# A one-core encoder block: three of five token tiles get their expert gates by one-hots instead of two, and four other rules of the order change

## The chip, the cores and the metric

The kernel runs on one core of one Trainium2 chip. The metric is the device time of one execution in microseconds, from the runs of the program on the chip; the profile is one more such execution, recorded by the hardware profiler. TensorE is PE here, VectorE DVE, ScalarE ACT, GpSimd POOL and SyncE SP, as the profile calls them.

## The reference, cut to what matters

One layer over 1,024 tokens of width 1,024. First a token-mixing sub-layer, then a layer of single-neuron experts, then a norm.

```python
n = modulate(rms_norm(h, g_norm1), shift1, scale1)
a_val, a_gate, u, v, gate_a, gate_b = split(n @ w_in)
z = conv_causal_31(a_val * sigmoid(a_gate)) + dw_b        # per channel
y_a = silu(layer_norm(z)) @ w_conv_out
mixed = einsum("gij,bnjgc->bnigc", w_masked, layer_norm(v)) + b_s
y_b = (u * mixed) @ w_sgu_out
h = h + gate1 * ((sigmoid(gate_a) * y_a + sigmoid(gate_b) * y_b) @ w_out)

n2 = modulate(rms_norm(h, g_norm2), shift2, scale2)
# 8 heads, 2 x 128 keys: top 16 of each half, top 16 of their sums
gate = softmax(s); e_idx = i1 * 128 + i2                  # 128 experts a token
a = einsum("td,tkd->tk", n2, expert_u[e_idx])
y = einsum("tk,tkd->td", gelu(a) * gate, expert_v[e_idx])
out = rms_norm(h + gate2 * y, g_final)
```

The shifts, scales and gates (`shift1` ... `gate2`) come from a small product of a conditioning row with `w_ada`, in twelve chunks of 512 columns.

## The kernel before, in words

**Tokens.** There are eight tiles of 128 tokens. The front half of the program runs over them in three blocks, of 3, 2 and 3 tiles (0 to 2, 3 and 4, 5 to 7). A block goes through a fixed list of weight products on PE, each of 24 matmuls of 128 x 128 weights with 384 or 256 token columns: for the first block `w_v`, then eight times `w_av`, `w_ag`, `w_u`; eight times `w_gb`, `w_sgu`; eight `w_ga`; eight `w_conv`; eight `w_out`. Then come the next block's `w_v`, and eight times the next block's `w_av`, `w_ag` and two of this block's 16 query products `w_q`, each followed by small score products. Weights are split into a high and a low part so that a float32 product takes three fast matmuls; the low part is made once, stored, and loaded again for the later blocks.

**The convolution** of a block is a generator (`conv`, held by `Conv`, line 961) that runs beside the products: 31 taps a channel tile on DVE (line 174), a mean over the channels by eight matmuls with `onesd`, a subtraction, squares, eight more such matmuls, a root, and then the swish and the split into high and low parts, which `w_conv` needs. In the last two blocks the last `NPT` = 4 taps of a channel tile are matmuls on PE with diagonal matrices `dg` that ACT makes.

**Experts.** Tiles 0 to 4 (`NDT` = 5) are dense: for each of 128 rows of 128 experts PE multiplies all 640 tokens by all experts' `expert_u`, DVE multiplies by a gate that is zero where the expert was not chosen, and PE multiplies by `expert_v`. Tiles 5 to 7 gather: for each token's 128 experts POOL gathers the rows of `expert_u` and then of `expert_v`, 384 + 384 gathers of 512 KB, and DVE makes 384 dot products and 384 scaled sums. The gathers run beside the dense part.

**Gates.** The dense tiles need their gates as a table, expert by token, in memory. `route` (line 341) finds a tile's 128 experts a token on DVE. For the first `NDD` = 3 tiles the table `g_a` is filled with zeros by SP, and `scatter` (line 554) lets POOL add the gates one column of 128 tokens at a time: 128 indirect transfers a tile, in 8 heads of 16, where a head waits for the landing of the tile's head before. The tiles' heads take turns. For the other `NOH` = 2 tiles the table is made by one-hots (class `Scatter`): 32 groups a tile, each of two comparisons and one product on DVE, twelve matmuls of 128 x 128 on PE (`pg`) and four copies on ACT, stored to `g_b`.

**What sets the order.** Nothing is scheduled by the chip or by a compiler: the program is written by a planner (`Plan`, line 60) that keeps a clock for each engine and records instructions as it goes. Work in the front line is recorded in program order. Tasks have a due time. Background generators (`pl.add`) are stepped in between the matmuls, the one with the lowest number first (`g[3]`: -1 free, 0 urgent, 1 the rest), as long as DVE's planned clock is not too far ahead. Each engine then takes its instructions strictly in the order they were recorded and waits on semaphores. SP takes nearly all loads and stores; in the last block's score products the last two stores go through POOL (`pl.late`).

**Other names.** `split_w` (line 669) casts a weight tile and calls for the next loads (`fetch_w`, `fetch_lo`). `mix_tables` loads the 128 x 128 mixing matrix `ws` and its bias row `tg` for one channel group. `ada` (line 741) makes one of the chunks of the conditioning product, in eight steps on DVE with four loads `aw`; chunks 6 to 9 must be done before the second norm's transposes. `routes` (line 1237) routes the tiles one after the other. `fence` waits for all scatters before the tables are read.

Of the kernel before, what the change touches and what calls it, by code (L numbers as in the profile page):

```python
# [9 lines left out]
BF16 = mybir.dt.bfloat16  # L10
I32 = mybir.dt.int32
# [19 lines left out]
BLOCKS = [(0,3),(3,2),(5,3)]  # L31
NDD = 3
TC = 32
# [13 lines left out]
NZ = 4  # L47
NPT = 4
LEAD = 1.0
# [252 lines left out]
def build(ctx, tc, I, O):  # L302
# [146 lines left out]
    class Scatter:  # L449
# [32 lines left out]
        def onehots(self, n):  # L482
# [3 lines left out]
            o1 = self.sb.tile([P, P, NTK], BF16, name="o1", tag="o1", bufs=2)  # L486
            o2 = self.sb.tile([P, P, NTK], BF16, name="o2", tag="o2", bufs=2)
            yield max([pl.ready(x, None, True) for x in (o1, o2)] + [pl.ready(iB), pl.ready(gB)])
# [75 lines left out]
    def scatter(gate, at):  # L564
# [6 lines left out]
        for h in range(H):  # L571
            now = []
            for k in range(h * K, (h + 1) * K):
# [7 lines left out]
                tc.add_to_no_dep_group("sc", i)  # L581
                pl.op("pool", 1.9, [], [gate, at])
                now.append(i)
# [85 lines left out]
    def split_w():  # L669
        if raws:  # L670
# [5 lines left out]
            def work():  # L676
                if old:
                    yield pl.ready(raw)
                    f = pl.acopy(hi, raw)
                    fetch_w()  # L680
                    fetch_lo()
                    yield max(f, pl.ready(lo))
                    return
# [280 lines left out]
    class Conv:  # L964


        def __init__(self, b, nn):
            self.N, self.nn = BLOCKS[b][1] * P, nn
            self.zs, self.done, self.free, self.out = {}, [], [], []
            self.zc = big("zc")  # L970
            self.gen = pl.add(conv(self.zc, self.zs, self.done, self.N, self.free, self.out, b + 1), True)

        def glu(self, j):
# [18 lines left out]
    def front(b, nn, v, cv):  # L992
# [26 lines left out]
        if b == 0:  # L1019
            cv = Conv(b, nn)  # L1020
        for j in range(J):
            if b == 0:
                cv.glu(j)
            tabs = mix_tables(j)
            pu = product(nh, nl, N)
            pend.append((j, pu) + tabs)
            if len(pend) > 1:
                pl.flush(1)
                mix(*pend.pop(0))
        pl.flush(1)  # L1030
        mix(*pend.pop(0))
# [210 lines left out]
    def routes():  # L1242
        for t in range(T // P):
            while t >= NDD and len(sct.routed) > 1 or len(heads) < min(t, NDD) - 3:
                yield pl.now + 1.0
            while t >= NDT and sct.made < NOH * sct.NQ:
                yield max(pl.now, pl.t["dve"]) + 1.0
            gate, i1f, i2f = r = [rp.tile([P, P], F32, name=n, tag=n, bufs=4 if n == "gate" else 2)
                                  for n in ("gate", "i1f", "i2f")]
            yield from route(rp, t, r)  # L1250
            if t < NDD:
                at = gsb.tile([P, P], I32, name="at", tag="at", bufs=4)
                pl.stt(i1f, i2f, float(P), i1f, OP.mult, OP.add)
# [461 lines left out]
```

## Time and profile before

| | |
|---|---|
| median of three runs | 3425.19 us (3420.99 to 3430.82) |
| the profiled execution's own time | 3423.22 us |
| its span from the first to the last instruction | 3421.1 us |
| PE busy | 3086.7 us, 90% |
| DVE busy | 2804.2 us, 82% |
| ACT busy | 1148.2 us, 34% |
| POOL busy | 1674.1 us, 49% |
| moved by DMA | 995.88 MB, 291 GB/s on average |

The front half ends and the dense half begins near 1,510 us. A busy time is a sum over the whole span; what a stage is worth is read from that stage. The busy time of PE is partly modelled, since its matmuls overlap. In a row of the profile `out<-in` names tiles, and in brackets stands how long the engine was idle ahead of it and what ended that.

### The profile page before, as it was taken

To read this page: it belongs to the slowest core of one execution; us is meant where nothing else is said; L and a number is where in the kernel's file an instruction comes from. 1 tells how busy PE (TensorE), PEld (TensorE's weight loads), DVE (VectorE), ACT (ScalarE), POOL (GpSimd) and SP (SyncE) were. 2 spreads that over 40 slices of the span, in tenths; PEclk is the share of its full clock that TensorE was granted. 3 is DMA by queue.
4 is the path that set the end of the run, shared out by engine and by line. 5 is a ranking of instruction groups with operands and counts; after the bars stand their busy time and mean duration, and the time that the engine had idled before them with its cause. 6 is when DMAs were issued, how large, how long until landed. Compare 5 with 4: busy or idle time off the path is not lost.

```text
span 3421.1 us, 49027 instructions
## 1 busy us (share of the span) xinstructions
PE 3086.7 (90%) x17598; PEld 2810.1 (82%) x17598; DVE 2804.2 (82%) x5741; ACT 1148.2 (34%) x1978; POOL 1674.1 (49%) x1549
## 2 busy tenths in 40 slices
PE   7969859888999969878999999999999999999991
PEld 4969749887798858777999999888889999999891
DVE  3799648777888847427999999899999998999998
ACT  4223444446543345533222222222222223222221
POOL 0000000027899999981232556566665554565663
PEclk9989989999999979989999999999999999999996
DMA  6969977879997758875676999999999998999997
GB/s 245 313 226 351 324 263 278 296 261 341 268 276 214 212 115 242 222 222 156 223 251 206 346 326 358 331 350 355 346 338 351 345 352 302 356 349 360 339 350 286
DMA packets 474036, 995.88 MB, mean 291 GB/s; under 512 B 87640, under 2 KB 247256, under 8 KB 473792
## 3 DMA queue, kind: packets, MB, share of 16 engines
q1 hardware_dynamic: 307776, 589.43, 49.7%
q0 software_dynamic: 166016, 403.32, 36.0%
q8 instruction: 138, 2.26, 0.3%
q14 instruction: 106, 0.87, 0.1%
HBM read 881.89 MB, written 110.71 MB: 290 GB/s over the span
## 4 chain that ended last, share of the span: by engine, by line
PE 36%; DVE 19%; DMA 18%; POOL 14%; issue 9%; ACT 3%; SPq 1%; DVEq 0%; ACTq 0%; POOLq 0%
PE ps L144 12%; POOL g_a L575 12%; PE pa L144 12%; PE pk L144 7%; DVE ya L174 6%; DMA raw<-in_v 5%; PE pr L144 5%; DMA w<-in_v,e 3%; DVE scr L174 2%; DVE yb L161 1%; DVE zc L174 1%; DVE vl L161 1%; DVE wlo L161 1%; DVE odd L174 1%; POOL w L1416 1%
## 5 line engine op out<-in xcount | busy, mean ns | idle before, releaser
L575 POOL DMA_INDIRECT g_a<-gate,at x384 | 654.9, 1705 | 842.3 <-DVE at L168 747.2
L1416 POOL DMA_INDIRECT w<-in_u,e x384 | 483.7, 1260 | 542.4 <-DVE scr L174 368.5
L144 PE MATMUL pa<-n2h,uh 128*128 128x320 f32 x2016 | 626.2, 311 | 39.6 <-ACT ge L195 37.3
L1416 POOL DMA_INDIRECT w<-in_v,e x384 | 485.5, 1264 | 343.1 <-DVE ya L174 243.4
L144 PE MATMUL pa<-n2l,uh 128*128 128x320 f32 x2016 | 625.9, 310 | 0.7 <-DVE n2l L161 0.7
L144 PE MATMUL pa<-n2h,ul 128*128 128x320 f32 x2016 | 625.9, 310 | 0.0
L174 DVE SCALAR_TENSOR_TENSOR ya<-w,aa,ya 128x1024 f32<-128x1024 f32 x381 | 489.1, 1284 | 23.7 <-DMA w<-in_v,e 18.3
L174 DVE SCALAR_TENSOR_TENSOR scr<-w,n 128x1024 bf16<-128x1024 f32 x384 | 469.3, 1222 | 12.1 <-DMA w<-in_u,e 4.6
L144 PEld LDWEIGHTS pa<-n2h,uh 128*128 128x128 f32 x2016 | 381.4, 189 | 52.5 <-ACT ge L195 40.8
L203 ACT CAST whi<-raw 128x1024 fp32r<-128x1024 f32 x264 | 276.7, 1049 | 387.4 <-PE ps L144 87.1
L144 PEld LDWEIGHTS pa<-n2l,uh 128*128 128x128 f32 x2016 | 381.2, 189 | 10.4 <-DVE n2l L161 1.1
L144 PEld LDWEIGHTS pa<-n2h,ul 128*128 128x128 f32 x2016 | 381.2, 189 | 0.0
L144 PE MATMUL ps<-nh,whi 128*128 128x384 f32 (+1 forms) x1024 | 352.1, 344 | 24.2 <-DVE z L161 10.7
L144 PE MATMUL ps<-nh,wlo 128*128 128x384 f32 (+1 forms) x1024 | 343.1, 335 | 7.8 <-DVE wlo L161 6.1
L144 PE MATMUL ps<-nl,whi 128*128 128x384 f32 (+1 forms) x1024 | 341.8, 334 | 1.6 <-DVE nl L161 1.6
L195 ACT ACTIVATE ge<-pa 128x320 f32<-128x320 f32 x249 | 108.6, 436 | 662.5 <-PE pa L144 662.5
L203 ACT CAST hh<-ge 128x320 fp32r<-128x320 f32 x250 | 115.0, 460 | 549.3 <-DVE ge L161 549.3
L144 PE MATMUL pk<-vh,hh 128*128 128x512 f32 x768 | 298.8, 389 | 0.0
L144 PE MATMUL pk<-vl,hh 128*128 128x512 f32 x768 | 298.8, 389 | 0.0
L144 PE MATMUL pk<-vh,hl 128*128 128x512 f32 x768 | 298.8, 389 | 0.0
L574 POOL MEMSET pad<- 128x1 f32 x384 | 274.3, 714 | 0.0
L144 PE MATMUL ps<-gh,whi 128*128 128x256 f32 (+1 forms) x704 | 223.8, 318 | 13.3 <-ACT gh L203 9.2
(252 smaller groups left out, 6663.1 us busy)
## 6 DMA issues: line engine op xcount, KB each, us to landing
raw<-in_uT SPq DMA_DIRECT2D x128, 512.0 KB
raw<-in_v SPq DMA_DIRECT2D x128, 512.0 KB
g_a<-zt SPq DMA_DIRECT2D x24, 1024.0 KB
raw<-in_w_q SPq DMA_DIRECT2D x48, 512.0 KB
gt<-g_a SPq DMA_DIRECT2D x32, 640.0 KB
aw<-in_w_ada SPq DMA_DIRECT2D x32, 512.0 KB
wlo<-lo_d_w_q SPq DMA_DIRECT2D x32, 512.0 KB
g_b<-st SPq DMA_DIRECT2D x32, 512.0 KB
```

Of the source, the lines that this page charges most:

```text
L144: self.nc.tensor.matmul(ps, w, x, start=start, stop=stop)
L161: self.nc.vector.tensor_tensor(out=out, in0=a, in1=b, op=op)
L174: self.nc.vector.scalar_tensor_tensor(out, a, s, b, op0=op0, op1=op1, **kw)
L195: self.nc.scalar.activation(out, a, func, **kw)
L203: self.nc.scalar.copy(out, a)
L574: nc.gpsimd.memset(pad, 0.0)
L575: i = nc.gpsimd.indirect_dma_start(out=g_1, out_offset=bass.IndirectOffsetOnAxis(ap=at[:, k:k + 1], axis=0), in_=gate[:, k:k + 1], in_offs ...
L1416: nc.gpsimd.indirect_dma_start(out=w, out_offset=None, in_=I["v" if ph else "u"], in_offset=bass.IndirectOffsetOnAxis(ap=ra[a][0][:, k:k + ...
```

## The change

Seven edits, in one diff:

- the gates of tiles 0 and 1 come by additions, those of tiles 2, 3 and 4 by one-hots (`NDD` 2, so `NOH` 3); the planner's price of one addition goes from 1.9 to 2.1, and `at` has two buffers instead of four;
- all 31 taps run on DVE in every block (`NPT` 0);
- one of the one-hot tiles, `o2`, has three buffers instead of two;
- where a weight's low part is loaded rather than made, the next loads are recorded when the planned cast has ended, and no longer with the cast;
- the background generators of the convolution, and of the routing from the second tile on, get the number 0.5 instead of 0;
- the mixing tables of group j + 1 are asked for after product j and before the next group's products.

```diff
-NDD = 3
+NDD = 2
...
-NPT = 4
+NPT = 0
...
-            o2 = self.sb.tile([P, P, NTK], BF16, name="o2", tag="o2", bufs=2)
+            o2 = self.sb.tile([P, P, NTK], BF16, name="o2", tag="o2", bufs=3)
...
-                pl.op("pool", 1.9, [], [gate, at])
+                pl.op("pool", 2.1, [], [gate, at])
...
                 if old:
                     yield pl.ready(raw)
-                    f = pl.acopy(hi, raw)
+                    yield pl.acopy(hi, raw)
                     fetch_w()
                     fetch_lo()
-                    yield max(f, pl.ready(lo))
+                    yield pl.ready(lo)
                     return
...
             self.gen = pl.add(conv(self.zc, self.zs, self.done, self.N, self.free, self.out, b + 1), True)
+            self.gen[3] = 0.5
...
+        tabs = mix_tables(0)
         for j in range(J):
             if b == 0:
                 cv.glu(j)
-            tabs = mix_tables(j)
             pu = product(nh, nl, N)
             pend.append((j, pu) + tabs)
             if len(pend) > 1:
                 pl.flush(1)
                 mix(*pend.pop(0))
+            if j + 1 < J:
+                tabs = mix_tables(j + 1)
...
+            rg[3] = 0.5 if t else 0
             yield from route(rp, t, r)
             if t < NDD:
-                at = gsb.tile([P, P], I32, name="at", tag="at", bufs=4)
+                at = gsb.tile([P, P], I32, name="at", tag="at", bufs=2)
```

The order that comes out differs in many places. Three of them follow.

PE, second block, where the first eight `onesd` matmuls of its convolution stand (`zc,onesd`). In this block `gh` and `gl` are the normed input's two parts. Before, they stand inside the product `w_gb4`:

```order
L144 MATMUL ps<-gh,whi 128x256
L144 MATMUL ps<-gl,whi 128x256
L144 MATMUL ps<-gh,wlo 128x256
L144 MATMUL ps<-zc,onesd 128x256 x8
L144 MATMUL ps<-gh,whi 128x256
```

Now they stand behind the last `w_ga` product, directly followed by the eight for the squares (`ts,onesd`), and the rows after those are `w_conv0`:

```order
L144 MATMUL ps<-gh,whi 128x256
L144 MATMUL ps<-gl,whi 128x256
L144 MATMUL ps<-gh,wlo 128x256
L144 MATMUL ps<-zc,onesd 128x256 x8
L144 MATMUL ps<-ts,onesd 128x256 x8
L144 MATMUL ps<-nh,whi 128x256
L144 MATMUL ps<-nl,whi 128x256
```

The tail of the convolution moved by 15 products, to the place where its result is wanted next. In the third block the matmuls for the squares moved in the same way, from `w_ga2` and `w_ga3` to the end of `w_ga7`.

PE, third block, in the query products, at the scores (`sk,qT`) between two of them. Before:

```order
L144 MATMUL ps_14724<-nl_14046,whi_14638 128x384
L144 MATMUL ps_14724<-nh_14045,wlo_14552 128x384
L144 MATMUL ps_14756<-sk_14502,qT_14719 128x128 x3
L144 MATMUL ps_14764<-nh_14045,whi_14681 128x384
L144 MATMUL ps_14764<-nl_14046,whi_14681 128x384
```

Now a group of twelve one-hot matmuls begins after the first matmuls of the product (its first two stand here):

```order
L144 MATMUL ps_15004<-sk_14593,qT_14865 128x128 x3
L144 MATMUL ps_15011<-nh_13575,whi_14733 128x384
L144 MATMUL ps_15011<-nl_13576,whi_14733 128x384
L144 MATMUL ps_15011<-nh_13575,wlo_14615 128x384
L144 LDWEIGHTS o2_14970
L144 MATMUL pg_15016<-so_15002,o2_14970 128x128
```

37 of the 96 groups now stand among the query products `w_q0` to `w_q11`, where none stood; 50 stand among `w_conv` and `w_out` (53 before), 5 among the second block's query products (none before), and 4 from `w_sgu4` to `w_ga7` (10, from `w_ga3` on, before; one more stood in the first `w_conv` and is counted in the 53).

DVE, third block, the write of tile 4's gates (`gate<-s,z`), with the semaphores it waits for; `DMASW` are those of POOL's transfers. Before, in product `w_ga3`, with one-hots of tile 3 ahead of it and behind it:

```order
L161 TENSOR_TENSOR o_11640<-iorep,iB 128x512
L161 TENSOR_TENSOR o_11641<-iorep,iB 128x512
L187 TENSOR_REDUCE z<-s 128x8 [waits Activation_49]
L183 RECIPROCAL z<-z 128x8 [waits DVE_49]
L161 TENSOR_TENSOR gate<-s,z 128x128 [waits DMASW4_49,DMASW3_49,DMASW5_49,DMASW2_49,DMASW6_49,DMASW1_49,DMASW7_49,DMASW0_49,DVE_49]
L161 TENSOR_TENSOR so<-o_11640,gB 128x1536
```

Now, in product `w_ga7`:

```order
L161 TENSOR_TENSOR s<-s,m 128x128 [waits DVE_49]
L187 TENSOR_REDUCE z<-s 128x8 [waits Activation_49]
L183 RECIPROCAL z<-z 128x8 [waits DVE_49]
L161 TENSOR_TENSOR gate<-s,z 128x128 [waits DMASW4_49,DMASW3_49,DMASW5_49,DMASW2_49,DMASW6_49,DMASW1_49,DMASW7_49,DMASW0_49,DVE_49]
L161 TENSOR_TENSOR so<-o_10872,gB 128x1536
```

The wait is still there: the four gate buffers go round, and tile 4 takes the one that tile 0's scatters read. It moved back by four products. In POOL's queue tile 0's last head is number 14 of 24 heads before (224 transfers with all before it) and number 12 of 16 now (192 transfers).

## Rows read from the trace of the kernel before

**Rows 1.** The chain of waits, first the stretch from 1100 to 1260 us, then from 1260 to 1560 us: its shares by line.

```profile
by line: POOL g_a L575 85.7%; issue 9.7%; POOL pad L574 6.2%
...
by line: POOL g_a L575 78.0%; issue 9.6%; POOL pad L574 5.6%; DMA g_a<-gate,at 2.4%; PE pa L144 1.8%; DMA sc_d<-so 1.1%; PE pr L144 0.7%; ACT L195 0.4%; ACT vh L203 0.3%; ACT ge L195 0.1%; ACTq L203 0.0%; POOLq L575 0.0%; POOLq L229 0.0%
```

**Rows 2.** Busy time by stretch: from and to, length, then busy us (and instructions) of PE, PE's weight loads, DVE, ACT and POOL, the granted clock of PE, the share of the DMA engines, GB/s.

```profile
857.00:1037.00 180.00, 172.14 (x1039) 157.79 (x1037) 150.60 (x446) 91.39 (x158) 162.16 (x156) 0.98 0.92 273
1037.00:1182.00 145.00, 137.78 (x761) 131.51 (x760) 129.34 (x522) 46.32 (x71) 131.03 (x150) 0.98 0.80 219
1182.00:1261.00 79.00, 40.35 (x256) 36.64 (x255) 26.91 (x55) 32.70 (x69) 71.36 (x84) 0.76 0.43 78
1261.00:1407.00 146.00, 144.84 (x987) 128.18 (x985) 106.14 (x199) 83.01 (x256) 132.41 (x148) 1.00 0.82 233
1425.00:1508.00 83.00, 79.57 (x468) 78.89 (x468) 18.04 (x71) 27.25 (x45) 74.80 (x88) 0.95 0.96 274
1508.00:1552.00 44.00, 12.03 (x62) 11.14 (x60) 11.82 (x27) 11.23 (x15) 30.97 (x36) 0.62 0.45 102
1552.00:1850.00 298.00, 295.20 (x1653) 269.20 (x1654) 278.75 (x892) 87.67 (x141) 61.87 (x53) 0.99 0.67 215
...
2050.00:2550.00 500.00, 489.09 (x2713) 442.64 (x2712) 459.32 (x634) 126.53 (x208) 309.14 (x238) 0.99 0.96 349
2550.00:3348.00 798.00, 794.33 (x4441) 721.84 (x4440) 749.01 (x968) 211.31 (x345) 464.69 (x369) 1.00 0.96 344
3348.00:3421.00 73.00, 2.06 (x9) 1.33 (x8) 59.99 (x59) 10.83 (x22) 27.82 (x23) 0.55 0.72 265
```

**Rows 3.** Who waited for whom between 1150 and 1260 us: engine, tile and line, what it waited for, us in total, times, the longest.

```profile
DVE gate L161 <- DMA g_a<-gate,at: 41.1, 1, 41.1
...
PE pg L144 <- DVE so L161: 38.6, 1, 38.6
```

**Rows 4.** The same between 1495 and 1600 us.

```profile
ACT vh L203 <- DMA sc_d<-so: 30.5, 1, 30.5
...
PE pa L144 <- ACT ge L195: 29.7, 1, 29.7
```

**Rows 5.** POOL in order of time, at its last scatter: start, length, engine, line, operation.

```profile
1544.58 1.56 POOL L575 DMA_INDIRECT g_a<-gate,at  x1 [0.19 <-issue]
1545.55 2.25 POOL L229 DMA_DIRECT2D sc_d<-so  x2
```

**Rows 6.** The instructions on the table `g_a`: shortest, median and longest in ns, first and last start.

```profile
L575 POOL DMA_INDIRECT g_a<-gate,at x384: 1556/1563/9224, 750.3 to 1544.6; - x192
```

**Rows 7.** POOL's instructions on `g_a` alone, by stretch: length, busy us (and how many), granted clock of PE, DMA share, GB/s.

```profile
750.00:850.00 100.00, 73.95 (x46) 0.97 1.01 331
850.00:950.00 100.00, 80.54 (x44) 0.97 0.92 275
950.00:1050.00 100.00, 86.78 (x44) 1.00 0.92 270
1050.00:1150.00 100.00, 84.45 (x52) 0.97 0.80 221
```

**Rows 8.** Groups of instructions between 1261 and 1407 us, in which 53 groups of one-hots ran: how many, busy us, mean ns of one, idle time ahead of them and what ended it.

```profile
L144 PE MATMUL pg<-so,o 128*128 128x128 bf16 x648 | 84.7, 297 | 0.8 <-DVE so L161 0.5 <-ACT st L203 0.3
...
L203 ACT COPY st<-pg 128x128 f32<-128x128 f32 x224 | 62.9, 441 | 48.2 <-PE pg L144 25.4 <-DMA g_b<-st 22.0 <-ACT st L203 0.3
...
L161 DVE TENSOR_TENSOR so<-o,gB 128x1536 bf16<-128x1536 bf16 x53 | 50.5, 954 | 0.0
L161 DVE TENSOR_TENSOR o<-iorep,iB 128x512 bf16<-128x512 bf16 x105 | 42.9, 423 | 30.1 <-PE pg L144 30.1
```

**Rows 9.** The instructions on `dg` alone, by stretch: length, busy us (and how many) of PE, PE's weight loads and ACT, then clock, DMA share and GB/s.

```profile
500.00:700.00 200.00, 13.22 (x56) 10.31 (x56) 10.21 (x32) 0.96 0.83 290
700.00:900.00 200.00, 1.89 (x8) 1.44 (x8) 0.00 (x0) 0.95 0.91 295
900.00:1160.00 260.00, 21.95 (x64) 11.82 (x64) 11.22 (x32) 0.99 0.87 250
```

**Rows 10.** Groups on DVE between 504 and 1160 us: half of the taps of a channel tile, with 384 and with 256 columns.

```profile
L174 DVE SCALAR_TENSOR_TENSOR zc<-z,cw,zc 128x384 f32<-128x384 f32 x104 | 63.8, 614 | 10.0 <-ACT zc L195 10.0
...
L174 DVE SCALAR_TENSOR_TENSOR zc<-z,cw,zc 128x256 f32<-128x256 f32 x104 | 49.9, 480 | 16.3 <-ACT zc L195 16.3
```

**Rows 11.** All engines in order of time at the end of the first block's convolution, behind its `w_ga7`; the last row is the first matmul of `w_conv0`.

```profile
338.80 5.32 PE L144 MATMUL ps<-zc,onesd 128*128 128x384 f32 x16
...
345.32 5.43 PE L144 MATMUL ps<-ts,onesd 128*128 128x384 f32 x16 [1.20 <-ACT ts L195]
...
351.40 2.55 DVE L183 RECIPROCAL ts<-ts 128x384 f32<-128x384 f32 x1 [3.43 <-ACT ts L195]
...
354.58 4.89 ACT L195 ACTIVATE zc<-zc,cols 128x384 f32<-128x384 f32 x8 [1.91 <-DVE zc L161]
...
359.93 0.69 PE L144 MATMUL ps<-gh,whi 128*128 128x384 f32 x1 [9.18 <-ACT gh L203]
```

**Rows 12.** DVE in order of time at the end of the first block: the end of chunk 8 of the conditioning product, the first and the last step of chunk 9.

```profile
443.88 0.16 DVE L174 SCALAR_TENSOR_TENSOR mcol<-ps,cols 128x4 f32<-128x4 f32 x1 [1.85 <-PE ps L154]
...
464.17 0.49 DVE L166 TENSOR_SCALAR acc<-aw,cT 128x512 f32<-128x512 f32 x1 [10.57 <-DMA aw<-in_w_ada]
...
474.23 0.16 DVE L174 SCALAR_TENSOR_TENSOR mcol<-ps,cols 128x4 f32<-128x4 f32 x1 [1.21 <-PE ps L154]
```

## The prediction, made before the changed kernel ran

> **What bounds the kernel now.** I read the chain of waits first, because it names the work that ends last. From 1100 us to 1551 us it runs almost wholly through POOL's scatters into `g_a` [rows 1]. Then I cut the span into stages [rows 2]. From 1261 us on, PE is busy 99% of most stretches, so a PE instruction added there costs its whole time. Two stretches stand out: 1182 to 1261 us, with PE busy 40.35 of 79 us, and 1508 to 1552 us, with 12.03 of 44 us. The waits tell why. In the first, DVE's gate of tile 4 waits 41.1 us for tile 0's scatters, which read the buffer it wants, and PE waits 38.6 us for the one-hot product queued behind it on DVE [rows 3]. In the second, ACT's `vh` waits 30.5 us for a store of scores, and PE 29.7 us for ACT [rows 4]; POOL issues that store only behind its last scatter, at 1545.55 us [rows 5]. Between 857 and 1182 us PE, weight loads, DVE and the DMA engines are all nearly full [rows 2]: 15 of 325 us is all PE has idle there. In the last 73 us PE is done; DVE works 60.0 us of them.
>
> So the kernel is bound by PE, with two holes of 68 us together that the additions make. The change takes a third of the additions away and gives PE matmuls for them.
>
> **The change part by part.** The sum goes by the profiled execution's 3423.2 us; the median of the runs is 2.0 us above it.
>
> *The wait for tile 4's gate.* The 384 transfers begin at 750.3 us [rows 6]; 186 are issued by 1150 us, then 0.52 a us [rows 7]. Tile 0's last is number 224: 38 more take 73 us, to 1223 us, and with a landing of 7.2 us (2.4% of the 300 us of chain, [rows 1]) 1230 us. The wait of 41.1 us before that began near 1189 us. Now the last is number 192: 6 more take 12 us, so it lands near 1169 us. DVE reaches the gate four products later; one product is 24 matmuls of three parts, 72 at 0.170 us (79.57 us by 468, [rows 2]), so 12 us, and even if only 16 us of work lies between, it is there near 1205 us. That leaves 36 us of margin: −38.6 us. Bounds: −44 (the slower clock, 0.76 mean in that stretch, comes back too) to −30 (a weight load or the norm is late next).
>
> *The store on POOL.* 256 transfers end 70 after number 186, that is 135 us after 1150, near 1285 us. Nothing stands ahead of the store when the scores are done: −29.7 us. Next late is the start of the dense loads, so −10 is the other bound; below −30 nothing can go.
>
> *One-hots for tile 2.* 32 groups more, each 12 matmuls. The 648 matmuls of such groups took 84.7 us beside other products, 0.131 us each [rows 8], where the count of loaded weights equals that of matmuls. So 32 × 12 × 0.131 = +50.2 us of PE. Is any of it hidden? 37 groups stand in the query products, where PE is busy 79.57 of 83 us [rows 2], so almost none. A group also takes 2 × 0.423 + 0.954 = 1.8 us of DVE and four copies of 0.28 us (62.9 us by 224) of ACT [rows 8]; for 37 groups 67 us of DVE and 41 us of ACT, in a stage where DVE had 18.0 and ACT 27.3 of 83 us [rows 2]. They fit beside PE, given that the stage grows by 58 us. Bounds: +25 if half goes into gaps of PE that the loads make (PE sits idle for 3 us of 83 while the DMA share is 0.96), +67 if the matmuls cost a third more among products whose weights also change each time. I take the row.
>
> *No taps on PE.* `dg` matmuls took 13.2, 1.9 and 22.0 us of PE [rows 9], 37 us. The 22.0 fall into the part from 900 us where PE paces: they go whole. Of the other 15.1 I count 3, because there PE waits for weights: −25 us. Bounds −37 to −10. On DVE, 32 taps more at 256 columns and 32 at 384 cost 32 × 0.480 + 32 × 0.614 = 35 us [rows 10]; DVE is busy 280 of the 325 us from 857 to 1182 us [rows 2], and loses ten groups' 18 us from that part, so they fit, if tightly.
>
> *The convolutions' tails.* In the second and third block the `onesd` matmuls now stand where the first block's stand: behind the last `w_ga`, with nothing recorded between them and `w_conv`. There PE was idle 1.20 us before the squares and 9.18 us before the first product [rows 11]. For 384 columns I take the 10, for 256 columns 8: +18 us. Bounds 0 (the rest of DVE's work happens to be done) to +28 (DVE is behind with the taps, and PE waits for the last of them).
>
> *Chunk 8 of the conditioning product.* Its loads stand later (from `w_out3` to `w_out7`), and its rest and chunk 9 are drained together before the second norm. The end of chunk 8 to the end of chunk 9 took 30 us, with 10.57 us of it for one load [rows 12]. Part of that lay there before; I take +8. Bounds 0 to +25.
>
> *The rest* I put at 0: eight zero fills fewer, the weight loads queued at the cast's end, the tables of one group ahead, the third `o2`, two `at`, the two generators' number, and the order of the gathers. The loads are off PE's chain where PE is 99% busy, and the stretch from 857 us can give back its 15 us at the most [rows 2]. Bounds: −25 (that, and 10 us of the first block) to +15 (the first weights arrive later behind what is queued ahead).
>
> Sum: −38.6 − 29.7 + 50.2 − 25 + 18 + 8 = −17.1, so 3406.1 us profiled and 3408 us as a median. Half the widths between the bounds (7, 10, 21, 14, 14, 12, 20) put together as independent errors, by the root of their squares, give 39 us if every one is at its bound; about half of that is my guess for most cases, so the forecast's own range is 3388 to 3428 us.
>
> **Rivals.**
>
> *1. The query products run at the one-hots' chain.* A group is a chain: comparisons and a product on DVE (1.8 us), matmuls, copies on ACT, and only three `o2`. PE takes the next group's matmuls in its order and stops if DVE has not finished. If PE waits the whole of DVE's 1.8 us in each of the 37 groups, 67 us come on top, 3475 us; with half, 3441 us. It decides from 0.46 us a group, which makes up the 17 us. Against it: with 53 groups in 146 us PE lost only 0.5 us to `so` and 0.3 us to `st` [rows 8]. For it: in that stretch the groups had products of 384 columns between them as here, but no score products with their copies on ACT. Chance 0.14.
>
> *2. The additions stay slow for longer, and the gate's wait survives.* They ran at 44 to 46 in 100 us up to 1050 us and at 52 after that [rows 7], and taps run on DVE while they are slow; with all taps on DVE that time lengthens. At 44 in 100 throughout, number 192 is issued at 750 + 436 = 1186 us and lands near 1194 us: still 11 us before DVE comes. Only at 41 in 100 (two tiles' heads in turn, not three, each waiting for its own tile's landing) is it 1218 us, landing near 1225 us, a wait of 20 us, 3428 us; in between, 3408 to 3428 us. Against it: 52 in 100 ran from 1050 us while DVE was 129 of 145 us busy [rows 2]. Chance 0.10. The Trainium skill, in "SBUF — State Buffer", section "Who interferes with whom", says that a DVE instruction with both inputs in SBUF contends with a GpSimd instruction that reads SBUF, and that the one behind stands still for the whole instruction of the other. The taps have two such inputs. By that rule all of the stretch with taps would go at the slow pace, which is the 44 in 100 above, so the rule alone leaves the forecast where it is; the trace's two paces agree with it but do not show that it is the cause.
>
> *3. The tail shrinks and the loads flow.* In the first 298 us of the dense half POOL issued only 53 instructions and the DMA share was 0.67; later it is 0.96 [rows 2]. The routing of tiles 6 and 7 moved far behind, so gathers can start at once. If those of the end have then landed before they are wanted, the tail falls from 73 us to DVE's 60.0 us in it, −13, and with the loads' 15 us of the stretch from 857 us it is 3380 us; with the tail alone 3395 us. Against it: 30 of 384 sums still stand behind the last dense piece, 31 before. Chance 0.13.
>
> **How the numbers follow.** Forecast 0.63, rivals 0.14, 0.10 and 0.13. A change of under 0.3%, 10.3 us, cannot be told from none, so faster is below 3414.9 us and slower above 3435.5 us. Of the forecast's 0.63 I put 0.41 below, 0.18 within and 0.04 above. Rival 1 gives 0.01 within and 0.13 above; rival 2 gives 0.03, 0.06 and 0.01; rival 3 gives 0.13 below. Together 0.57 faster, 0.25 same, 0.18 slower. The range for 8 times in 10 takes in rival 3's 3380 us and rival 1's half case: 3374 to 3442 us.
>
> **What would show it.** Right: no wait of `gate` on `g_a` above 5 us; no wait of `vh` on `sc_d`; the last scatter before 1300 us; the front half's end some 15 us earlier, the dense part and the tail unchanged; PE's `pg` matmuls some 50 us longer in sum; near 10 us of idle PE before each `w_conv0`. Rival 1 shows as PE waiting for `so` or `st` in the query products; rival 2 as the wait of `gate` left over; rival 3 as a tail under 65 us. The forecast fails above all if DVE, with 35 us more taps, falls behind from 857 to 1182 us: then PE waits for the convolution's tail far longer than 10 us and the gain is gone.

## The result, and the profile after

The changed kernel takes 3407.49 us (median of 8 runs, 3396.44 to 3418.14), the kernel before in the same set 3424.66 us (8 runs). The ratio is 0.9949, with a 95% interval of 0.9931 to 0.9967. The profiled execution's span is 3405.0 us, 16.1 us less than the 3421.1 us of before. The prediction was 3408 us and "faster".

A sum can be right with wrong terms, so the first question is where in the program the 16.1 us came up. The two traces have the same list of weight products, and the start of each product's first matmul can be laid side by side. The table is worked out from the PE rows of both traces. The last column says what lies in the step and, in brackets, what the prediction had put there. Its terms are PE's time from the start of a matmul to the start of the next one, with idle time counted by itself; the `onesd` matmuls in it are those of the convolutions' tails, which stand in a later step than before.

| start of | before, us | after, us | after − before | step, and the prediction's term |
|---|---|---|---|---|
| 5th `w_v` of the second block | 482.2 | 501.2 | +18.9 | chunk 8 drained: +19, of it idle +13 (+8) |
| first `w_ga`, second block | 768.9 | 767.3 | −1.6 | −20: `dg` gone −12, `onesd` moved on −6, other −2 (0) |
| first `w_conv`, second block | 795.2 | 807.4 | +12.2 | +14: `onesd` moved here +7, PE idle behind the tail +7 (+8) |
| first `w_u`, third block | 1036.9 | 1047.7 | +10.8 | −1: 5 groups added +7, `dg` gone −11, slower matmuls behind the tail +4 |
| first `w_ga`, third block | 1168.6 | 1165.4 | −3.2 | −14: `dg` gone −7, `onesd` moved on −5, other −2 |
| fifth `w_ga` | 1234.0 | 1187.2 | −46.8 | −44: gate's wait −39 (−38.6), 3 groups fewer −4 |
| first `w_conv` | 1260.7 | 1222.2 | −38.5 | +8: PE idle behind the tail +9 (+10), `onesd` moved here +5, 4 groups fewer −5 |
| first `w_q` | 1424.7 | 1381.6 | −43.1 | 4 groups fewer: −5 |
| end of the last `w_q` | 1508.3 | 1514.3 | +6.0 | 37 groups: +50 (+58), PE idle −2 |
| 379th `pa` matmul of the dense half | 1671.8 | 1649.7 | −22.1 | store's wait: −28 (−29.7) |
| end of PE's work | 3350.1 | 3333.1 | −17.0 | dense half: +5 (0) |
| end of the span | 3421.1 | 3405.0 | −16.0 | tail: +1 (0) |

The rows of after that answer to [rows 2] show the same. Columns as there: length, busy us (and instructions) of PE, weight loads, DVE, ACT and POOL, clock, DMA share, GB/s.

```profile
1182.00:1261.00 79.00, 70.23 (x420) 64.95 (x419) 58.16 (x119) 44.96 (x93) 63.25 (x71) 0.94 0.67 178
1261.00:1407.00 146.00, 131.40 (x876) 115.04 (x876) 103.82 (x194) 84.43 (x247) 42.42 (x47) 0.94 0.68 222
1382.00:1514.00 132.00, 130.38 (x915) 123.87 (x915) 75.53 (x179) 69.14 (x207) 0.00 (x0) 0.98 0.71 251
1508.00:1552.00 44.00, 39.55 (x243) 38.08 (x241) 33.52 (x160) 18.62 (x29) 1.75 (x3) 0.92 0.69 224
1552.00:1850.00 298.00, 295.55 (x1637) 268.01 (x1638) 277.23 (x520) 85.06 (x136) 144.45 (x118) 0.99 0.88 311
...
3332.00:3405.00 73.00, 1.08 (x5) 0.56 (x3) 56.71 (x55) 8.81 (x19) 26.11 (x22) 0.54 0.69 252
```

In both holes of before PE is now busy: 70 of 79 us where it had 40, and 39.55 of 44 where it had 12. The tail has the length it had, though POOL now issues 118 instructions instead of 53 in the first 298 us of the dense half.

The summary of the tile `g_a` in the changed kernel, to be held against [rows 6] and [rows 3]: shortest, median and longest in ns, first and last start; below, who waited for it (us, times).

```profile
L575 POOL DMA_INDIRECT g_a<-gate,at x256: 1556/1564/7636, 747.2 to 1310.7; - x128
...
  POOL g_a L575: 29.9, 7
  DVE gate L161: 0.2, 1
```

The wait of 41.1 us is 0.2 us, and those are the checks of four pairs of semaphores at 0.05 us each: by the trace's semaphore updates number 192, the last of tile 0, had landed at 1175.0 us, and DVE came to the gate at 1204.4 us. The last addition starts at 1310.7 us, 11 us later than the sign that the prediction had set (before 1300 us; POOL waited 29.9 us for landings between the heads), but that is over 200 us before the dense half begins. Of the waits between 1495 and 1600 us, against [rows 4]:

```profile
POOL sc_d L229 <- ACT so L203: 203.6, 1, 203.6
...
DVE ul L161 <- ACT uh L203: 20.3, 1, 20.3
ACT qT L203 <- PE ps L144: 15.9, 5, 3.7
ACT ge L195 <- PE pa L144: 13.5, 3, 5.8
ACT vh L203 <- DMA raw<-in_v: 11.6, 3, 10.2
```

POOL now stands ready for 203.6 us before the scores come; nobody waits for the store.

The query products, 1382 to 1514 us, by groups of instructions (count, busy us, mean ns of one, idle time ahead and what ended it), against [rows 8]:

```profile
L144 PE MATMUL pg<-so,o 128*128 128x128 bf16 x444 | 58.0, 297 | 0.0
...
L203 ACT COPY st<-pg 128x128 f32<-128x128 f32 x158 | 44.3, 443 | 40.0 <-DMA g_b<-st 20.5 <-PE pg L144 19.5
...
L161 DVE TENSOR_TENSOR so<-o,gB 128x1536 bf16<-128x1536 bf16 x36 | 34.4, 957 | 32.6 <-PE pg L144 30.2 <-ACT gB L203 2.4
L161 DVE TENSOR_TENSOR o<-iorep,iB 128x512 bf16<-128x512 bf16 x70 | 26.4, 419 | 0.0
```

444 matmuls are 37 groups; 58.0 us by 444 is 0.131 us, to the digit the price taken from [rows 8]. But a busy time counts the modelled end of a group's last matmul, while the next matmul has already started. From start to start a one-hot matmul makes PE's queue longer by 0.113 us here (50.3 us for the 444) and by 0.112 us in the 648 of [rows 8] (72.7 us; 648 matmuls are 54 groups, one more than the 53 counted there). PE never waits for a one-hot there; it is DVE that waits for PE, 30.2 us.

The idle PE that the prediction expected ahead of the first `w_conv`, in order of time for the second block and then the third:

```profile
796.55 3.72 PE L144 MATMUL ps<-ts,onesd 128*128 128x256 f32 x16 [0.96 <-ACT ts L195]
807.45 0.58 PE L144 MATMUL ps<-nh,whi 128*128 128x256 f32 x1 [7.17 <-ACT nh L203]
```

```profile
1222.22 0.69 PE L144 MATMUL ps<-gh,whi 128*128 128x384 f32 x1 [8.77 <-ACT gh L203]
```

And chunks 8 and 9 of the conditioning product, each of which PE now waits for before the second norm; in the kernel before, whose row comes first, it waited there for chunk 9 alone:

```profile
470.22 2.08 PE L144 MATMUL ps<-acc,ones 128*128 128x512 f32 x2 [13.36 <-DVE acc L174]
```

```profile
461.63 2.08 PE L144 MATMUL ps<-acc,ones 128*128 128x512 f32 x2 [15.56 <-DVE acc L174]
...
482.38 2.07 PE L144 MATMUL ps<-acc,ones 128*128 128x512 f32 x2 [16.77 <-DVE acc L174]
```

### The profile page after: what moved, and what is told of

It is laid out like the page before. It is cut to its first block, busy times and chain, and to the rows that moved or that the text cites. A ratio compares the mean times of both kernels' runs of the same rounds, so it can differ in the third digit from the quotient of the medians.

```text
span 3405.0 us, 49599 instructions
## 1 busy us (share of the span) xinstructions
PE 3108.5 (91%) x17857; PEld 2831.7 (83%) x17857; DVE 2886.0 (85%) x5888; ACT 1159.3 (34%) x2042; POOL 1471.6 (43%) x1293
## 4 chain that ended last, share of the span: by engine, by line
PE 53%; DMA 18%; DVE 17%; issue 6%; ACT 3%; POOL 1%; SPq 1%; DVEq 0%; ACTq 0%; POOLq 0%
PE ps L144 18%; PE pa L144 16%; PE pk L144 9%; PE pr L144 6%; PE pg L144 4%; DVE ya L174 4%; DMA raw<-in_v 4%; DMA w<-in_v,e 2%; DVE scr L174 2%; DMA w<-in_u,e 1%; DVE wlo L161 1%; DMA raw<-in_w_out 1%; DVE zc L174 1%; ACT whi L203 1%; DVE vl L161 1%
## 5 line engine op out<-in xcount | busy, mean ns | idle before, releaser
L575 POOL DMA_INDIRECT g_a<-gate,at x256 | 458.7, 1792 | 819.5 <-DVE at L168 744.1
L144 PE MATMUL pa<-n2h,uh 128*128 128x320 f32 x2016 | 625.0, 310 | 12.3 <-ACT ge L195 10.1
L144 PEld LDWEIGHTS pa<-n2h,uh 128*128 128x128 f32 x2016 | 380.5, 189 | 24.5 <-ACT ge L195 12.6
L144 PE MATMUL ps<-gh,wlo 128*128 128x256 f32 (+1 forms) x704 | 219.5, 312 | 18.7 <-DMA wlo<-lo_d_w_ag 12.7
```

Of the source, the lines that this page charges most:

```text
L144: self.nc.tensor.matmul(ps, w, x, start=start, stop=stop)
L575: i = nc.gpsimd.indirect_dma_start(out=g_1, out_offset=bass.IndirectOffsetOnAxis(ap=at[:, k:k + 1], axis=0), in_=gate[:, k:k + 1], in_offs ...
```

## The experiments

Theory A reads the prediction's terms in one way: the additions of before are one chain whose end sets the dense half's start, and once it is short PE's own work sets the time. (The prediction itself had counted the two waits as separate terms, which is theory B of e1.) Its rivals are named in each expectation. All ratios are to the kernel before in the same set of runs, with 95% intervals.

### The two waits: one chain or two

**e1**, before with five gate buffers:

```diff
-bufs=4 if n == "gate" else 2
+bufs=5 if n == "gate" else 2
-at = gsb.tile([P, P], I32, name="at", tag="at", bufs=4)
+at = gsb.tile([P, P], I32, name="at", tag="at", bufs=3)
```

> The kernel before with five gate buffers instead of four (and three at instead of four, to make room); no other instruction moves. Theory A (one chain): the additions on POOL run to 1551 us whatever PE does, and the dense half cannot start before them, so the 38 us that PE no longer waits at tile 4's gate come back as a longer wait at the dense half's start: vh waits some 65 to 70 us for its store instead of 30.5, the total stays at 3425 (3420 to 3430). Theory B (two separate waits, each worth its length): 38 us are gained, 3386 (3380 to 3392).

Measured: 3428.09 us, ratio 0.9997 (0.9984 to 1.0009). Its waits between 1450 and 1600 us:

```profile
ACT vh L203 <- DMA sc_d<-so: 57.3, 1, 57.3
...
PE pa L144 <- ACT ge L195: 56.6, 1, 56.6
```

The gate's wait is gone and PE is busy 78.83 us of the 79 us from 1182 us. The query products end at 1481.1 us, 27 us earlier than before; PE's wait grew from 29.7 to 56.6 us, and the 379th `pa` matmul of the dense half starts at 1671.8 us, the same tenth of a microsecond as in the kernel before. Theory B is refuted: the two waits are one chain met in two places.

**e9**, e1 and the last two score stores on SP:

```diff
-pl.late = not nxt
+pl.late = False
```

> The kernel before with five gate buffers (and three at), as e1, and in addition the last two score stores on SP instead of POOL, so that they stand behind no addition; PE's order of products and groups is that of before. In e1 vh waited 57.3 us for that store and nothing was gained. Theory A (one chain: the dense half needs the tables, and so the end of the additions, near 1547 us): the wait moves to the loads of g_a, and only the work that fits ahead of them is gained, 10 to 25 us: 3410 (3403 to 3418). Theory B (the store's place in POOL's queue is the second wait, worth its length): 57 us are gained, 3371 (3365 to 3380).

Measured: 3407.3 us, ratio 0.9936 (0.9916 to 0.9957). The waits:

```profile
ACT hh L203 <- DVE ge L161: 34.2, 3, 31.6
...
PE pr L144 <- issue: 32.6, 1, 32.6
DVE ge L161 <- DMA gt<-g_a: 30.1, 1, 30.1
```

As theory A had it, the wait moved on to the load of the tables `gt`, which follows the last addition; theory B's 57 us did not come. But what fitted ahead of it was worth 19 us. So the store's place behind the additions in POOL's queue did have a price of its own, about a third of the 57.3 us of waiting; and a version without any new one-hot reaches the time of the changed kernel.

### The parts one at a time

**e3**, before with `NDD` 2 and nothing else.

> The kernel before with two tiles by additions and three by one-hots, and nothing else. Theory A (the sum of the prediction): -38.6 for the gate's wait, -29.7 for the store, +50.2 for 32 groups, nothing for taps, tails or chunk 8: 3407 (3400 to 3413), no wait of gate above 5 us, no wait of vh on the store. Theory C (the gain is that of the other edits; one-hots only exchange a wait for work): 3425 or more.

Measured: 3420.16 us, ratio 0.9973 (0.9956 to 0.9991): faster, by less than theory A's 18 us. Both waits are gone as expected. The expectation had left out the conditioning chunk, which it need not have: the fifth `w_v` of the second block starts 24 us later than before, 15 us of that are still there at the second block's first `w_u` and 12 us at its first `w_ga`. That is about the difference to theory A. 12 groups stand in the second block's `w_q` products.

**e2**, before with `NPT` 0 and nothing else.

> The kernel before with no taps on PE (NPT 0), still three tiles by additions. Theory A (one chain): 25 us less of PE work lie ahead of the end of the additions, which stays near 1550 us, so the waits take them back and the total stays at 3425 (3419 to 3430). Theory B (PE's work counts wherever PE paces): -25 for the matmuls, +10 for the convolution's tail of the third block, now behind the last w_ga: 3410 (3400 to 3415).

Measured: 3455.1 us, ratio 1.0063 (1.0042 to 1.0085), slower, where neither theory had it. The tile `g_a` says why:

```profile
L575 POOL DMA_INDIRECT g_a<-gate,at x384: 1555/1564/9757, 770.3 to 1568.2; - x192
```

The taps stand ahead of the first tile's routing on DVE, so the additions begin 20 us later and end 23.6 us later, and the total follows. That is the chain again, and a mistake in the expectation: it took the chain's start as given.

**e4**, before with both `NDD` 2 and `NPT` 0, without the five smaller edits.

> The kernel before with NDD 2 and NPT 0 and none of the other five edits. The convolution's tail of the second block now stands before the end of w_ga, that of the third at its end as in the changed kernel. Theory A: -18 for the one-hots, -25 for the dg matmuls, +10 for one drained tail, +8 for chunk 8: 3400 (3393 to 3407), that is 8 to 14 us less than the changed kernel. Theory C (the small edits carry a part of the gain): more than the changed kernel's 3407, up to 3420.

Measured: 3408.61 us, ratio 0.9932 (0.9912 to 0.9952), against 0.9949 of the changed kernel. With two tiles by additions the five smaller edits together move nothing that can be seen. Theory A's 8 to 14 us below the changed kernel did not show either: from the second block's first `w_ga` to its first `w_conv` e4 takes 6 us less, but at that `w_ga` it stands 6 us further back, 4 us of it because 20 of the trace's 32 rows of `onesd` matmuls of this tail already stand ahead of it.

**e10**, e2 and the number 0.5 for the two generators:

```diff
+            self.gen[3] = 0.5
...
+            rg[3] = 0.5 if t else 0
```

> The kernel of e2 (before without taps on PE, three tiles by additions; 3455, its additions began at 770.3 us and ended at 1568 us) with one more edit of the change: the generators of the convolution and of the routing from the second tile on get the number 0.5, so that the first tile's routing goes ahead of the taps. Theory A (one chain: the time is the additions' start plus their length): they begin near 742 us as in e7, 28 us earlier, and the total falls by 28 to 50 us, to 3405 to 3427. Theory C (the loads' place, the tables or the price of an addition did it in e7): 3450 to 3458 as e2.

Measured: 3441.11 us, ratio 1.0036 (1.0025 to 1.0047). The additions:

```profile
L575 POOL DMA_INDIRECT g_a<-gate,at x384: 1557/1565/7644, 757.3 to 1551.9; - x192
```

They begin 13 us earlier than in e2, not 28, and the time falls by 14 us (by the two ratios, 9). The edit does what theory A says, through the additions' start, but half as much as I had read out of e7.

**e7**, the changed kernel with three tiles by additions again.

```diff
-NDD = 2
+NDD = 3
...
-at = gsb.tile([P, P], I32, name="at", tag="at", bufs=2)
+at = gsb.tile([P, P], I32, name="at", tag="at", bufs=3)
```

> The changed kernel with three tiles by additions and two by one-hots again (and three at, which that needs), all other edits kept. Theory A (one chain of 384 additions, its end is its start plus 794 us): the additions begin near 750 to 770 us, so they end between 1545 and 1565 us and the total is 3425 to 3447, slower than the changed kernel by 18 us or more. Theory C (the gain is that of the other edits): 3407 or less, since 32 groups of 1.57 us are gone.

Measured: 3400.33 us, ratio 0.9923 (0.9906 to 0.9940): not slower than the changed kernel, so theory A's number failed by 25 us and more, and theory C's (3407 or less) came true: without any new one-hot the other edits bring at least as much as all of them together. Two rows of this kernel explain it, the additions and the end of POOL's queue in order of time:

```profile
L575 POOL DMA_INDIRECT g_a<-gate,at x384: 1554/1557/7637, 741.9 to 1532.5; - x192
```

```profile
1500.45 1.56 POOL L575 DMA_INDIRECT g_a<-gate,at  x1 [0.19 <-issue]
1501.42 2.22 POOL L229 DMA_DIRECT2D sc_d<-so  x2
1503.06 0.69 POOL L574 MEMSET pad<- 128x1 f32 x1
1504.15 1.70 POOL L575 DMA_INDIRECT g_a<-gate,at  x1 [0.40 <-issue]
```

The additions begin 8 us before those of the kernel before and end 12 us before them, and the store no longer stands behind the last one but is issued 31 us ahead of it, with a cover of additions behind. So the dense half starts while additions still run, as in e9. The chain stands, but its last link differs. No run tells which of the edits that e7 has beyond e10 moves the store ahead and the additions' start from 757.3 to 741.9 us. The span less the start of the last addition is the test:

| kernel | last addition starts, us | span, us | difference |
|---|---|---|---|
| before | 1544.6 | 3421.1 | 1876.5 |
| e1 | 1543.9 | 3421.5 | 1877.6 |
| e2 | 1568.2 | 3453.3 | 1885.1 |
| e10 | 1551.9 | 3432.5 | 1880.6 |
| e9, store on SP | 1543.4 | 3405.8 | 1862.4 |
| e7, store ahead of the last additions | 1532.5 | 3400.8 | 1868.3 |
| after, two tiles | 1310.7 | 3405.0 | 2094.3 |

Where the store is last in POOL's queue, the end follows the last addition within 9 us while that moves by 24 us. Where it is not, it is 8 to 23 us less. In the changed kernel the additions set nothing any more.

### What the work in place of the waits costs

**e5**, the changed kernel with `NPT` 4.

> The changed kernel with the last four taps on PE again (NPT 4). No tail of the second or third block's convolution is then drained between w_ga and w_conv, and 32 groups of one-hots stand in the second block's query products. Theory A (the prediction's terms): +25 us for dg, -18 us for the two tails that are covered again: 3414 (3408 to 3421). Theory B (PE had room for dg beside the weight loads, so only the tails count): 3389 (3383 to 3396).

Measured: 3402.53 us, ratio 0.9932 (0.9915 to 0.9948): between the theories. Taking the taps off PE shows no gain once the waits are gone. At the third block's first `w_ga` e5 is 54.5 us behind the changed kernel, with 31 us of `dg`, 35 us for 26 more groups and 5 us of `onesd` matmuls more ahead of it, counted from start to start; against that PE was idle 14 us less (151 us up to there, 166 in the changed kernel). At the end of the last `w_q`, where the changed kernel has made its 37 groups and e5 none, it is 2.5 us behind, and at the end of PE's work 6 us ahead.

**e6**, the changed kernel with the convolution's generator at 0 (the line `self.gen[3] = 0.5` left out).

> The changed kernel with the convolution's generator at number 0 again, so that its steps are recorded first: both onesd tails stand early, and DVE's taps stand ahead of routing and one-hots. Theory A (PE stands idle some 18 to 20 us behind the two drained tails, and that is all they cost): 3388 (3382 to 3395). Theory D (DVE is full from 857 to 1182 us, so what the taps take first the gates get later, and PE waits there instead): 3407 (3400 to 3415).

Measured: 3398.16 us, ratio 0.9918 (0.9900 to 0.9937): half of theory A's 20 us. The waits behind both tails are gone (in the second block PE waits 6.5 us for low parts of weights instead); but the third block's first `w_ga` starts at 1185.7 us, 20 us later than in the changed kernel, with 8 more groups of one-hots (11 us) and 9 us of earlier `onesd` matmuls ahead of it, and the additions slow down (below). At the end of the last `w_q` e6 is 12 us ahead.

**e12**, both of these.

> The changed kernel with both of e5 and e6: four taps on PE again and the convolution's generator at number 0, so that no tail is drained and no group of one-hots is left for the last query products. Theory A (the two are separate costs, the taps on DVE worth 5 us as e5 measured, the drained tails 9 us as e6 measured): 3393 (3388 to 3399), faster than every kernel so far. Theory G (e5 and e6 removed the same cost, PE's wait for a DVE that has more to do than PE between 780 and 1230 us): 3398 to 3403, no better than the better of the two.

Measured: 3400.87 us, ratio 0.9911 (0.9886 to 0.9936). The median lies in theory G's range, but its six runs go from 3388 to 3407 us, and the interval reaches theory A's 3393 us too (0.990 of before). The trace leans to theory G: PE's idle time up to the end of the last `w_q` is 189 us in the changed kernel, 167 in e5, 172 in e6 and 163 here, so 26 us less, where the two by themselves make 22 and 17. That the one cost is DVE's having more to do than fits beside PE from 780 to 1230 us is argued, not shown.

**e8**, the changed kernel with the next loads recorded with the cast.

```diff
-                    yield pl.acopy(hi, raw)
+                    f = pl.acopy(hi, raw)
                     fetch_w()
                     fetch_lo()
-                    yield pl.ready(lo)
+                    yield max(f, pl.ready(lo))
```

> The changed kernel with the next loads recorded with the cast again; this moves the recorded order much: 53 groups of one-hots in the last query products (37 in the changed kernel), 39 in w_conv and w_out (50), and both tails drained. Theory A (a group costs PE the same 1.4 to 1.6 us wherever PE paces): 3407 (3401 to 3413). Theory E (groups in the query products cost more than in w_conv and w_out, because DVE's chain of 1.8 us a group shows there): 16 groups by some 0.5 us and more, 3415 to 3425.

Measured: 3421.97 us, ratio 0.9984 (0.9970 to 0.9998). The time is theory E's, but not for its reason. The group's price in the query products, and the waits of PE from 845 to 915 us:

```profile
L144 PE MATMUL pg<-so,o 128*128 128x128 bf16 x636 | 83.1, 297 | 1.4 <-ACT st L203 1.4
```

```profile
PE ps L144 <- DMA wlo<-lo_d_w_out: 14.2, 2, 8.6
```

636 matmuls in 83.1 us are 0.131 us each, as everywhere. What is lost is a wait of 14.2 us for low parts of `w_out`, which the changed kernel does not have there, though it has others (from the second block's first `w_conv` to the third's first `w_av` e8 takes 8 us longer), and 5 us at the dense half's start. So theory E's chain is out; the rest of the difference I did not trace. So the place of the loads does matter in one product; with e4, which also has the old place and loses nothing, I don't call it a property of the rule.

**e11**, the changed kernel with the conditioning chunks at number 0.

```diff
-ada_todo.append(pl.add(rest_of_ada(i, chs)))
+ada_todo.append(pl.add(rest_of_ada(i, chs), True))
```

> The changed kernel with the generator of the conditioning chunks at number 0: their products are made earlier, and chunk 8 and 9 are no longer drained together before the second norm; groups, tails and taps stand where they stood. Theory A (the 19 us that PE falls behind at the first Nw_v products are mostly given back, since the weight loads set the pace behind them): 3402 (3398 to 3407). Theory F (the stall counts whole): 3388 (3384 to 3393).

Measured: 3413.7 us, ratio 0.9964 (0.9950 to 0.9978): no gain, and neither theory's number. The edit did not take the stall away but moved it. The chunks' work now stands in the first block, whose first `w_conv` starts at 415.2 us instead of 359.7 with PE idle 92 us up to there instead of 52 (16.4 us of it a wait for DVE's `zc`); at the second norm PE is idle 7 us instead of 36, and up to the end of the last `w_q` 190 us against 189. So the run does not tell how much of a stall is given back. e3 tells more: there the taps stand as in the kernel before, and of the 24 us at chunk 8 half was gone by 780 us. That the loads set the pace there would fit it, and no run tested it by itself.

## Why the prediction was right, step by step

**The gate's wait** (−38.6) was right: PE's 38.6 us of waiting are gone, and of the step's other 5 us 4 are one-hots that now stand elsewhere. Tile 0's last addition landed at 1175.0 us and DVE came at 1204.4 us, where the prediction had 1169 and 1205. Rival 2 is out, though its pace showed for a while: 39 additions in 100 us from 950 us on, 51 in the next 100. One reckoning was wrong and did no harm: a product is 24 matmuls, 4.1 us at 0.170 us, not 72 and 12 us; the 16 us that the prediction took as the least is what four products take.

**The store** (−29.7) was right in size, −28.1. But the step that counted it as a wait separate from the gate's was right only because both were cut at once: e1 shows that the first alone is worth nothing, and e9 that the additions, not the store alone, hold the dense half back.

**The one-hots** (+50.2) were put 7 us too high. The row's 0.131 us came again, but the queue grows by the 0.113 us from start to start: 86.2 us for the 768 matmuls of before, 129.8 us for 1152, which is +43.6. The stage of the query products grew by 49 us, 50.3 for the one-hots with 1.8 us less of idle time. Rival 1 is out: DVE waits for PE there.

**The taps** (−25): PE's queue lost 30.6 us of `dg` matmuls, 18.3 of them from the third block's first `w_av` on (the prediction's 22) and 12.3 before, of which it had counted 3. That little of the latter is a gain fits e7, which has no `dg` and no delay at chunk 8: at the second block's first `w_ga` it is 8.1 us ahead of the kernel before, and 6.3 us of that are `onesd` matmuls that come later. As a gain of the edit the 25 us are not there: e5, with the taps on PE, is no slower than the changed kernel (0.9932 against 0.9949), since PE is idle 22 us less in it up to the end of the last `w_q`, 9 us of that at the two tails.

**The tails** (+18) were right in size: PE is idle 8.1 and 8.8 us in the rows above. What the sum left out is that the matmuls behind such a wait are slower: the second block's first `w_conv` product took 5.1 us instead of 3.0. After the 7.2 us in which PE was idle its granted clock was 0.50 from 807 to 811.5 us, the lower of its two levels (1.2 GHz), and 0.99 from 811.5 to 815 us; in the kernel before it was 1.00 from 795 to 803 us.

**Chunk 8** (+8) was +19 at first. Of that a part was given back: of e3's 24 us 12 were left at the second block's first `w_ga`, and of the 17 us by which the changed kernel is behind e7 at the fifth `w_v` 7 were left there. So the term was right in size, without a reckoning behind it.

**The rest** (0): the dense half lost 5 us that the prediction had not, 3.8 of them idle time of PE, and the tail of the program was 72 us, 71 before. Rival 3 is out, in spite of the earlier gathers.

**The sum.** PE's time up to the end of the last `w_q`, from start to start, and what follows:

| us | before | after | after − before | prediction |
|---|---|---|---|---|
| PE idle | 203.6 | 189.0 | −14.6 | −38.6 + 18 + 8 = −12.6 |
| one-hot matmuls | 86.2 | 129.8 | +43.6 | +50.2 |
| `dg` matmuls | 30.6 | 0 | −30.6 | −25 |
| all other matmuls | 1187.9 | 1195.5 | +7.6 | 0 |
| to the end of the last `w_q` | 1508.3 | 1514.3 | +6.0 | +12.6 |
| from there to the end | 1912.8 | 1890.7 | −22.1 | −29.7 |

The mechanism was right in the main, and no line of this table is off by more than 8 us. That the total came within 1 us is luck: the front part came out 7 us shorter than the terms make it, and the dense part with its end 8 us longer.

What the prediction did not see is that the change had a cheaper neighbour: with the other edits alone (e7) the time is 3400 us. The 32 groups exchange waits for work of nearly the same length, and once the store stands ahead of the last additions they bring nothing that the runs show. The fastest in ratio are e12 at 0.9911, e6 at 0.9918 and e7 at 0.9923. Their intervals overlap with each other and, by a little, with the changed kernel's, so they are probably faster, by some 7 to 13 us, but that is not shown beyond the noise, nor which is best.

## What to carry to other kernels

Two waits in a profile that hang on the same queue may be one: find the queue's last item, and ask what moves if the first wait is cut alone. Work that replaces a wait is paid in full where the engine already paces; take its price from start to start (0.113 us a one-hot matmul here), not from a busy time that counts overlap (0.131 us). Of a stall early in the program about half was given back here. Before a step between two time marks is given to one cause, count which instructions have moved across the marks. An instruction that others wait for should stand ahead of a late queue's last items, or on another queue.

## What the runs showed of the hardware

The additions slow down while DVE runs taps. Here are POOL's instructions on `g_a` from 950 to 1050 us in the changed kernel and then in e6 (length, busy us and count, clock, DMA share, GB/s), with DVE's on the taps' line in the same 100 us behind each.

```profile
950.00:1050.00 100.00, 88.40 (x39) 1.00 0.95 296
```

```profile
950.00:1050.00 100.00, 73.51 (x137) 1.00 0.95 296
```

```profile
950.00:1050.00 100.00, 91.16 (x30) 1.00 0.96 312
```

```profile
950.00:1050.00 100.00, 82.00 (x154) 1.00 0.96 312
```

In the kernel before there were 44 additions [rows 7] beside 58.20 us of that line. So there were 44, 39 and 30 additions in 100 us at 58, 74 and 82 us of DVE's work. An addition is longer, not only rarer: 88.40 by 39 is 2.27 us, where in the next 100 us, with 38.18 us on the taps' line, it is 84.49 by 51, 1.66 us:

```profile
1050.00:1150.00 100.00, 84.49 (x51) 0.98 0.84 232
```

The Trainium skill, in "SBUF — State Buffer", section "Who interferes with whom", says that a DVE instruction with two SBUF inputs contends with a GpSimd instruction that reads SBUF. The traces agree in direction, with three amounts; that a shared port is the cause no run here tested. The amount of taps alone does not give the pace: from 850 to 950 us the changed kernel has 14.85 us of that line, and an addition takes 82.00 by 45, 1.82 us. Full DMA engines alone don't do it: in the kernel before, from 750 to 850 us, the DMA share was 1.01 and an addition took 73.95 by 46, 1.61 us [rows 7]. What the long additions have in common is seen one by one. Here is one of the changed kernel and one of e6, each followed by the tap on DVE that ends an unbroken run of taps and by the instruction behind it:

```profile
1018.78 7.64 POOL L575 DMA_INDIRECT g_a<-gate,at  x1 [0.19 <-issue]
...
1024.36 0.61 DVE L174 SCALAR_TENSOR_TENSOR zc<-z,cw,zc 128x384 f32<-128x384 f32 x1
1024.89 0.17 DVE L179 COPY z<-ztail 128x30 f32<-128x30 f32 x1
```

```profile
935.89 13.46 POOL L575 DMA_INDIRECT g_a<-gate,at  x1 [0.19 <-issue]
...
947.31 0.61 DVE L174 SCALAR_TENSOR_TENSOR zc<-z,cw,zc 128x384 f32<-128x384 f32 x1
947.84 0.17 DVE L179 COPY z<-ztail 128x30 f32<-128x30 f32 x1
```

Both end 1.5 us after the run is broken, and 1.56 us is the median of an addition. So do all seven additions of the changed kernel that took over 3 us (3.40 to 7.64 us): each ended 1.40 to 1.52 us after the first DVE instruction that is not a tap. They stood still until then, and e6, which records up to 22 taps in a row behind an addition's start, has the longest. Not every addition is caught: 61 of the changed kernel's 256 began during a tap, and 10 of these took over 2.3 us. What decides that is open.

It cost the changed kernel nothing, because the gate had 29 us to spare; it would cost a kernel whose additions are the chain.
